# A decoder trunk on one core: modulation sums placed elsewhere

## The chip, the core and the metric

The kernel runs on one core of a Trainium2 chip. The metric is the device time of one execution in microseconds. Engines are named as in the profile: PE is TensorE, DVE is VectorE, ACT is ScalarE, POOL is GpSimd, SP is SyncE, which issues the DMAs here.

## The reference

Two layers on x of 256 rows by 1024. Each layer has a token mixer and a channel mixer, each of them with a modulation that is computed from one vector c:

```
mod = silu(c) @ w_ada[l] + b_ada[l]          # 1024 x 6144, split into sh1, sc1, g1, sh2, sc2, g2
h = x * (1 + sc1) + sh1
m = token_mixer(h)                           # h @ w_in (2816 columns: q k v hq hf hi hg pu), attention,
                                             # gated recurrence, causal pooling, then @ w_out
x = layer_norm(ALPHA * x + (1 + g1) * m) * ln1_g + ln1_b
h = x * (1 + sc2) + sh2
f = swiglu(h) (layer 0: FFN 2816)  or  moe(h) (layer 1: 8 experts of 3584, top 2)
x = layer_norm(ALPHA * x + (1 + g2) * f) * ln2_g + ln2_b
```

## The kernel before

The stages follow one another: mixer 1, dense SwiGLU, mixer 2, router, experts. The 256 rows are two blocks of 128 (NB = 2).

**Matmuls in fp32.** Each weight tile of 1 MB lands in a `raw` tile and is split by `split_half` into a high part `wh` (ScalarE, line 208) and a low part `wl` (line 209, on GpSimd or VectorE by the pattern LSUB). The input of a projection, `hT`, is split too (lines 313 and 314). Three matmuls make a product: high by high, high by low (lines 353 and 354 in the mixers, 924 and 925 in the dense stage) and low by high (356 and 927).

**The ring.** All weights come through `raw_tile`, a ring of RAW = 5 tiles (10 more where a mixer closes and during the experts), issued on SyncE's queue in program order (line 188). A tile is issued when its slot is free.

**Modulation pieces.** A piece is 512 columns of w_ada: two raw tiles (`ada_load`), eight matmuls on TensorE that sum them with the condition as stationary operand (line 270), a copy or an addition of the bias row on VectorE (lines 275 and 277), and then either four one-column matmuls that turn the sum into columns (`ada_cols`, line 283, with a small addition on VectorE, line 285), or one matmul that spreads it over the partitions and a ScalarE copy (`ada_gate_half`, lines 292 and 293). A sub-layer needs four shift and scale pieces (`queue_mod`) ahead of it and two gate pieces (`queue_gate`) behind it. The queue `bg` holds them, and `background(n)` takes n of them at that point of the program. In the mixers the points are given by BG (after the v, hv and u projections) and TURNS (turns of the loop over attention, projection and recurrence threads); in the dense stage FB = 2 are taken after each of the six chunks of the hidden width (256 and five of 512).

**First input.** `first_input(hf)` makes the input of mixer 1 for one half of the 1024 channels: two pieces, the affine coefficients, and `to_hT`, which transposes x (four 128x128 transposes per block, line 337), applies the affine step on ScalarE (line 342) and splits the result on VectorE. Two projections, f (columns from 1536) and q (from 0), take their steps between the halves; order on VectorE, ScalarE and TensorE is as written there (`manual_schedule`). Elsewhere a scheduler with its own costs sets each engine's order within the limits of the tiles and of `issue_after`, which puts an instruction behind another one of the same engine.

**Norms.** `resid_norm` adds the residual (lines 816 and 817), makes statistics, takes the reciprocal root on GpSimd (line 808) and normalises x in place on VectorE (line 822). Then the transposes of the next input follow. The norm's own scale and shift are folded into the affine coefficients for that input; for the residual path `new_x` applies them to x itself, two GpSimd rows per block (lines 855 and 856), behind the last reciprocal root.

## Time and profile before

| | |
|---|---|
| timed runs, median | 1532.04 us (1531.99, 1532.04, 1533.95) |
| profiled execution | 1529.82 us, span 1527.6 us |
| mean granted clock of TensorE | 0.944 |
| busy over the span | PE 91%, DVE 29%, ACT 21%, POOL 18% |
| mixer 1, with first input | 0 to 206.6 us |
| dense stage | 224.8 to 463.4 us |
| mixer 2 | 472.5 to 628.4 us |
| router, then experts | from 628.4 and 647.6 us |

A row of a timeline gives the start, the duration, the engine and line, what is written from what, and in brackets how long the engine idled before it and what released it. "wh", "wl" and "raw" are the weight tiles above, "acc" the sum of a piece, "rt" a half of `hT`, "bnrs" the reciprocal root. In tables by windows each engine's busy time is followed by its count of instructions; PE clock is the granted TensorE clock as a share of full speed (2.4 GHz; 0.5 is 1.2 GHz).

### The profile page before, as it was taken

How to read it: one execution, taken by the hardware profiler on the slowest of the kernel's cores; microseconds unless marked ns; L12 is line 12 of the kernel's file. 1: busy time of each engine (PE TensorE's matmuls, PEld its weight loads, DVE VectorE, ACT ScalarE, POOL GpSimd, SP SyncE). 2: the span in 40 equal slices, each digit the busy share in tenths (PEclk: the TensorE clock that was granted, in tenths of full speed). 3: DMA queues.
4: the chain of work that ended last, by engine and by line, in shares of the span. 5: the costliest groups of instructions: out<-in, count | busy, mean ns of one | idle time of the engine just before them, and what ended most of it. 6: DMA issues, size and time to landing. Idle time of an engine off the chain costs nothing.

```text
span 1527.6 us, 20906 instructions
## 1 busy us (share of the span) xinstructions
PE 1383.4 (91%) x8612; PEld 791.1 (52%) x8612; DVE 440.0 (29%) x748; ACT 320.2 (21%) x579; POOL 276.8 (18%) x154
## 2 busy tenths in 40 slices
PE   6889969999997988899978899899988999999994
PEld 3657758887875766743324344354434443435332
DVE  2555672322347656620000300002001200000303
ACT  2444434323324543211000100010000000001000
POOL 3443154544445532120000000000000000000001
PEclk7989989999998999899988799999999999999998
DMA  9756337766673532699999999999999999999994
GB/s 327 280 166 240 102 125 278 273 248 241 248 264 130 183 123 101 248 376 356 409 408 396 409 409 408 407 404 408 409 402 402 409 409 397 408 389 406 404 402 173
DMA packets 161094, 480.34 MB, mean 314 GB/s; under 512 B 9304, under 2 KB 14936, under 8 KB 160992
## 3 DMA queue, kind: packets, MB, share of 16 engines
q1 hardware_dynamic: 160992, 478.94, 82.2%
q8 instruction: 69, 1.13, 0.3%
q14 instruction: 33, 0.27, 0.0%
HBM read 477.86 MB, written 1.05 MB: 314 GB/s over the span
## 4 chain that ended last, share of the span: by engine, by line
issue 55%; PE 3%; POOL 1%; DMA 1%; DVE 0%; ACT 0%; POOLq 0%; DVEq 0%; ACTq 0%
PE psu L1206 1%; DMA raw<-in_ln_g_dram 1%; PE psx L1131 0%; PE pa L356 0%; PE pa L354 0%; PE pa L353 0%; POOL xa L1325 0%; PE pc L1034 0%; POOL xa L1323 0%; POOL rs L808 0%; ACT raw L1466 0%; DVE Sb L1122 0%; DVE off L1461 0%; ACT g L1041 0%; PE pb L1031 0%
## 5 line engine op out<-in xcount | busy, mean ns | idle before, releaser
L1206 PE MATMUL psu<-raw,xs 128*32 128x256 f32 (+4 forms) x3776 | 500.4, 432 | 21.0 <-DMA raw<-in_exp_w_dram 21.0
L1206 PEld LDWEIGHTS psu<-raw,xs 128*32 128x32 f32 (+2 forms) x3776 | 210.9, 127 | 298.5 <-issue 225.3
L209 POOL TENSOR_TENSOR wl<-raw,wh 128x1024 fp32r<-128x1024 f32 (+1 forms) x82 | 193.5, 2370 | 228.4 <-ACT wh L208 212.7
L1244 PE MATMUL psx<-raw,gT 128*32 128x512 f32 (+1 forms) x896 | 162.0, 636 | 15.0 <-DMA raw<-in_exp_w_dram 15.0
L208 ACT ACTIVATE wh<-raw 128x1024 fp32r<-128x1024 f32 (+1 forms) x130 | 131.2, 1033 | 192.6 <-DMA raw<-in_ffn_w_dram 78.8
L808 POOL TENSOR_TENSOR rs<-rs,mhalf 128x1 f32<-128x1 f32 x2 | 2.4, 1193 | 830.7 <-DVE rs L807 830.7
L353 PE MATMUL pa<-wh,rt 128*128 128x512 f32 (+1 forms) x296 | 119.2, 406 | 8.3 <-ACT wh L208 6.6
L354 PE MATMUL pa<-wh,rt 128*128 128x512 f32 (+1 forms) x296 | 116.6, 397 | 2.7 <-DVE rt L314 2.7
L209 DVE TENSOR_TENSOR wl<-raw,wh 128x1024 fp32r<-128x1024 f32 (+1 forms) x48 | 75.5, 1572 | 109.7 <-ACT wh L208 109.7
L1244 PE MATMUL psx<-raw,gTb 128*128 128x512 f32 x224 | 103.2, 612 | 1.1 <-DMA raw<-in_exp_w_dram 1.1
L356 PE MATMUL pa<-wl,rt 128*128 128x512 f32 (+1 forms) x296 | 100.2, 397 | 0.8 <-POOL wl L209 0.8
L1218 DVE TENSOR_TENSOR g<-g,psu 128x256 f32<-128x256 f32 (+2 forms) x32 | 15.2, 476 | 277.3 <-PE psu L1206 141.6
L1244 PEld LDWEIGHTS psx<-raw,gT 128*32 128x32 f32 (+1 forms) x896 | 37.8, 123 | 108.8 <-issue 87.3
L1214 ACT ACTIVATE g<-psu 128x256 f32<-128x256 f32 (+2 forms) x32 | 13.7, 427 | 302.8 <-PE psu L1206 302.8
L1244 PEld LDWEIGHTS psx<-raw,gTb 128*128 128x128 f32 x224 | 42.0, 194 | 60.1 <-issue 56.5
L353 PEld LDWEIGHTS pa<-wh,rt 128*128 128x128 f32 x296 | 58.7, 199 | 22.9 <-ACT wh L208 7.2
L1218 DVE TENSOR_TENSOR gb<-gb,psu 128x512 f32<-128x512 f32 x14 | 9.6, 688 | 211.5 <-PE psu L1206 211.5
L354 PEld LDWEIGHTS pa<-wh,rt 128*128 128x128 f32 x296 | 58.7, 198 | 14.1 <-DVE rt L314 3.9
L356 PEld LDWEIGHTS pa<-wl,rt 128*128 128x128 f32 x296 | 55.8, 197 | 14.0 <-POOL wl L209 2.3
L1229 ACT ACTIVATE gT<-psx 128x256 f32<-128x256 f32 (+2 forms) x32 | 13.6, 427 | 211.5 <-PE psx L1228 176.3
L924 PE MATMUL pb<-rt,wh 128*128 128x256 f32 x176 | 48.8, 298 | 9.3 <-DVE rt L313 6.8
L270 PE MATMUL pb<-raw,condw 128*32 128x512 f32 x384 | 49.0, 625 | 5.6 <-DMA raw<-in_w_ada_dram 5.6
(299 smaller groups left out, 1551.2 us busy)
## 6 DMA issues: line engine op xcount, KB each, us to landing
raw<-in_exp_w_dram SPq DMA_DIRECT2D x336, 1024.0 KB, 17.6
raw<-in_w_ada_dram SPq DMA_DIRECT2D x48, 1024.0 KB, 5.7
raw<-in_ffn_w_dram SPq DMA_DIRECT2D x31, 1024.0 KB, 6.9
raw<-in_w_in_dram SPq DMA_DIRECT2D x22, 1024.0 KB, 6.9
raw<-in_w_out_dram SPq DMA_DIRECT2D x8, 1024.0 KB, 5.0
raw<-in_ffn_w_dram SPq DMA_DIRECT2D x4, 512.0 KB, 4.8
t<-in_cst_dram SPq DMA_DIRECT2D x8, 192.0 KB, 2.5
x<-in_x_dram SPq DMA_DIRECT2D x2, 512.0 KB
```

The lines of the kernel that those rows point to most:

```text
L208: hl["act"] = act(h, ri, AF.Copy)
L209: hl["sub", eng] = (G if eng else V).tensor_tensor(l, ri, h.bitcast(F32), op=ALU.subtract)
L270: mm(ps[32 * j:32 * j + 32], condw[:, k, :], raws[k // 4][:, j, :], start=k < 4, stop=k >= 4)
L353: mm(ps, lH(a), rH(w), start=first and i == 0, stop=False)
L354: mm(ps, lL(a), rH(w), start=False, stop=False)
L356: mm(ps, lH(a), rL(w), start=False, stop=last and i == n - 1)
L924: mm(o_, wH[:, k, js], hT.H(4 * h + k0 + k, full), start=h + k0 + k == 0, stop=False)
L1206: mm(ps[self.rows(j)], self.of.xs[:, k0 + k, :], wv[:, k, o:o + w], start=k0 + k == 0, stop=k0 + k == KD - 1)
L1214: act(self.g[:, s_ * 512:s_ * 512 + min(512, self.F)], ps, AF.Silu)
L1218: V.tensor_mul(g, g, ps)
L1229: act(self.gT[:, b0:b0 + m, :], pt.rearrange("p (b s) -> p b s", b=m), AF.Copy)
L1244: mm(ps[self.rows(c)], self.gT[:, b, self.rows(j)], wv[:, i, hf * 512:hf * 512 + 512], start=seq == 0, stop=seq == n - 1)
```

## The change

There are three parts.

1. `first_input` is cut into four functions: load, sums, turn (transposes into the ps_c banks, which `to_hT` then reads) and apply. `mixer` calls them between single steps of the f and q projections; `proj(..., apart=True)` stops once after the load and split of its tiles.
2. `new_x` no longer issues its rows but puts the four of them into the queue `slow`; `aside()` takes one from it, on each odd turn of a mixer's loop and once before each of the 11 later column groups of the dense stage.
3. The dense stage takes one piece before its loop and one per chunk from the second on, between the w1 and the w3 matmuls, instead of two after each chunk. The pieces of gate 1 and of the second sub-layer of layer 1 are queued in mixer 2, which takes them by its BG and by five new TURNS; the last gate piece is left for the point after mixer 2.

```diff
--- before.py
+++ after.py
@@ -48,8 +48,7 @@
 
 
 BG = (0, 1, 0, 1)
-TURNS = ((10, 19, 20), ())
-FB = 2
+TURNS = ((10, 19, 20), (8, 12, 16, 19, 20))
 ORDER = "paprar"
 OUTORDER = ((0,), (1,), (3, 2))
 
@@ -329,12 +328,15 @@
         def L(self, k, s):
             return self.l[k // 4][:, k % 4, s]
 
-    def to_hT(src, AB_, dst, b, hf, after=None):
-
-        A, B = AB_
-        ps = ps_b()
+    def turned(src, hf, ps):
         for j in range(4):
             tr(ps[:, j * P:(j + 1) * P], src[:, (hf * 4 + j) * P:(hf * 4 + j + 1) * P], ident)
+        return ps
+
+    def to_hT(src, AB_, dst, b, hf, after=None, ps=None):
+
+        A, B = AB_
+        ps = ps or turned(src, hf, ps_b())
         bs = slice(b * P, (b + 1) * P)
         v = t2().rearrange("p (a t) -> p a t", a=4)
         for j in range(4):
@@ -417,7 +419,14 @@
         V.tensor_scalar(dst, ss, 1.0 / n, EPS, op0=ALU.mult, op1=ALU.add)
         G.tensor_tensor(dst, dst, mhalf[:, :dst.shape[1]], op=ALU.pow)
 
-    bg = []
+    bg, slow = [], []
+
+    def aside(n=1):
+
+        for _ in range(n):
+            if slow:
+                with tc.issue_after(hl["normed"].ins):
+                    slow.pop(0)()
 
     def background(n=1):
 
@@ -430,12 +439,16 @@
 
         W = w_in[l]
 
-        def proj(c0, n, ps):
+        def proj(c0, n, ps, apart=False):
+
 
             ps += [ps_a() for _ in range(NB)]
             pieces = [(0, lambda: piece(W, 0, D, c0, n))] if n == 256 else [(4 * h, lambda h=h: col_half(W, c0, n, h)) for h in range(2)]
             for h, load in pieces:
-                for k0, kk, wH, wL in load():
+                ws = load()
+                if apart:
+                    yield
+                for k0, kk, wH, wL in ws:
                     for b in range(NB):
                         part(ps[b], n, b, h + k0, kk, wH, wL)
                     yield
@@ -457,14 +470,26 @@
         psf, psq, psk, psv, psh, psu_ = [], [], [], [], [], []
         if inputs:
             with tc.manual_schedule(engines={E.DVE, E.Activation, E.PE}):
-                steps = [proj(1536, 512, psf), proj(0, 512, psq)]
-                for h in range(2):
-                    last = inputs(h)
-                    for g in steps:
-                        next(g)
-                        next(g)
-                for g in steps:
-                    run(g)
+                f_, q_ = proj(1536, 512, psf, True), proj(0, 512, psq, True)
+                load, sums, turn, apply_ = inputs
+                raws = load(0)
+                sums(0, 0, raws)
+                next(f_)
+                sums(0, 1, raws, turn)
+                apply_(0)
+                next(q_)
+                raws = load(1)
+                next(f_)
+                next(f_)
+                sums(1, 0, raws)
+                next(q_)
+                sums(1, 1, raws, turn)
+                next(q_)
+                apply_(1)
+                next(f_)
+                next(q_)
+                run(f_)
+                run(q_)
         else:
             psf += [ps_a() for _ in range(NB)]
             subs = [(4 * h + w[0],) + w[1:] for h in range(2) for w in col_half(W, 1536, 512, h)]
@@ -744,6 +769,8 @@
         while threads:
             for t_ in ORDER:
                 background(TURNS[l].count(turn))
+                if turn % 2:
+                    aside()
                 turn += 1
                 if t_ in threads and next(threads[t_], threads) is threads:
                     del threads[t_]
@@ -850,10 +877,9 @@
 
     def new_x(gb):
 
-        with tc.issue_after(row_stats.last.ins):
-            for b in range(NB):
-                G.tensor_tensor(x_t[b], x_t[b], gb[0], op=ALU.mult)
-                G.tensor_tensor(x_t[b], x_t[b], gb[1], op=ALU.add)
+        for b in range(NB):
+            for a, op in zip(gb, (ALU.mult, ALU.add)):
+                slow.append(lambda b=b, a=a, op=op: G.tensor_tensor(x_t[b], x_t[b], a, op=op))
 
     def queue_mod(l, sub, gk, bk):
         def go(which, hf):
@@ -878,18 +904,31 @@
 
     hT = Act()
 
-    def first_input(hf):
-        hT.new(hf)
-        for which in (1, 0):
-            ada_cols(0, which, hf, ada_acc(ada_load(0, which * D + hf * 512)))
+    def first_load(hf):
+        raws = [ada_load(0, which * D + hf * 512) for which in (1, 0)]
         if hf == 0:
             for b in range(NB):
                 nc.sync.dma_start(x_t[b], x[0, b * P:(b + 1) * P, :])
+        return raws
+
+    first_ps = []
+
+    def first_turn(hf):
+        hT.new(hf)
+        first_ps[:] = [turned(x_t[b], hf, ps_c()) for b in range(NB)]
+
+    def first_sums(hf, i, raws, between=None):
+        acc = ada_acc(raws[i])
+        if between:
+            between(hf)
+        ada_cols(0, 1 - i, hf, acc)
+
+    def first_apply(hf):
         affine_half(0, 0, None, None, hf)
         for b in range(NB):
-            last = to_hT(x_t[b], AB[0, 0], hT, b, hf)
-        return last
-
+            to_hT(None, AB[0, 0], hT, b, hf, ps=first_ps[b])
+
+    first_input = first_load, first_sums, first_turn, first_apply
     gate1 = queue_gate(0, 2)
     queue_mod(0, 1, LN["g1", 0], LN["b1", 0])
     acc = mixer(0, hT, first_input)
@@ -905,8 +944,7 @@
     hl["ph"] = 1
     gate2 = queue_gate(0, 5)
     queue_mod(1, 0, LN["g2", 0], LN["b2", 0])
-    gate1_ = queue_gate(1, 2)
-    queue_mod(1, 1, LN["g1", 1], LN["b1", 1])
+    background()
     yacc = [[ps_a() for _ in range(2)] for _ in range(NB)]
     full = slice(0, T)
     widths = [256] + [512] * (FFN // 512)
@@ -915,6 +953,10 @@
         nj = n // P
         pu = [(ps_b, ps_c)[j % 2]() for j in range(nj)]
         for wi, w in enumerate((ffn_w1, ffn_w3)):
+            if fc and wi:
+                background()
+            if fc + wi:
+                aside()
             for h in range(2):
                 for k0, kk, wH, wL in col_half(w[0], f0, n, h):
                     for j in range(nj):
@@ -952,7 +994,6 @@
         downs.append(down)
         if fc:
             downs.pop(0)()
-        background(FB)
         f0 += n
     downs.pop(0)()
     background(9)
@@ -964,6 +1005,8 @@
     new_x(gb)
 
     hl["ph"] = 2
+    gate1_ = queue_gate(1, 2)
+    queue_mod(1, 1, LN["g1", 1], LN["b1", 1])
     gate2 = queue_gate(1, 5)
     acc = mixer(1, hT)
     background(9)
```

In the rows below, taken from the order in which each engine's instructions stand, a line number of the changed kernel is that of the same code 1 lower in the pieces (269 for 270, 282 for 283) and 2 higher in the projections (355 for 353, 358 for 356).

The first place is TensorE in mixer 1, the end of the first projection steps, where the second half of the input is made. "raw,condw" is the sum of a piece, "quad,acc" its turn into columns, "cp,x" a transpose of x. Before:

```order
L356 MATMUL pa<-wl,rt 128x512 x2
L270 MATMUL pb<-raw,condw 32x512 x8
L283 MATMUL pb<-quad,acc 128x1 x4
L270 MATMUL pb<-raw,condw 32x512 x8
L283 MATMUL pb<-quad,acc 128x1 x4
L337 MATMUL pb<-cp,x_73 128x128 x4
L337 MATMUL pb<-cp,x_74 128x128 x4
L353 MATMUL pa<-wh,rt 128x512
L354 MATMUL pa<-wh,rt 128x512
L353 MATMUL pa<-wh,rt 128x512
L354 MATMUL pa<-wh,rt 128x512
```

After, from the fourth group of the first half:

```order
L358 MATMUL pa<-wl,rt 128x512 x2
L269 MATMUL pb<-raw,condw 32x512 x8
L282 MATMUL pb<-quad,acc 128x1 x4
L355 MATMUL pa<-wh,rt 128x512
L356 MATMUL pa<-wh,rt 128x512
```

and from the end of that step:

```order
L358 MATMUL pa<-wl,rt 128x512 x2
L269 MATMUL pb<-raw,condw 32x512 x8
L333 MATMUL pc<-cp,x_73 128x128 x4
L333 MATMUL pc<-cp,x_74 128x128 x4
L282 MATMUL pb<-quad,acc 128x1 x4
L355 MATMUL pa<-wh,rt 128x512
L356 MATMUL pa<-wh,rt 128x512
```

Before, the two sums, the two turns and the eight transposes stand together; after, four groups of projection matmuls (rows not shown between the two pieces) stand between the first sum and the second, and the transposes stand before the second turn, into the ps_c banks.

The second place is GpSimd from the dense stage to mixer 2. "bnrs" is a block's reciprocal root, x0 and x1 are the two blocks, t4 the rows of scale and shift, "wl" a low part of a weight tile. Before:

```order
L209 TENSOR_TENSOR wl_3631<-raw_3624,wh_3630 128x1024
L209 TENSOR_TENSOR wl_3773<-raw_3770,wh_3772 128x1024
L808 TENSOR_TENSOR bnrs_3699<-bnrs_3699,mhalf_87 128x1
L209 TENSOR_TENSOR wl_3783<-raw_3780,wh_3782 128x1024
L808 TENSOR_TENSOR bnrs_3736<-bnrs_3736,mhalf_87 128x1
L855 TENSOR_TENSOR x0_73<-x0_73,t4_3682 128x1024
L856 TENSOR_TENSOR x0_73<-x0_73,t4_3684 128x1024
L855 TENSOR_TENSOR x1_74<-x1_74,t4_3682 128x1024
L856 TENSOR_TENSOR x1_74<-x1_74,t4_3684 128x1024
L209 TENSOR_TENSOR wl_3843<-raw_3840,wh_3842 128x1024
```

After:

```order
L208 TENSOR_TENSOR wl_3502<-raw_3495,wh_3501 128x1024
L835 TENSOR_TENSOR bnrs_3570<-bnrs_3570,mhalf_87 128x1
L208 TENSOR_TENSOR wl_3640<-raw_3637,wh_3639 128x1024
L208 TENSOR_TENSOR wl_3650<-raw_3647,wh_3649 128x1024
L882 TENSOR_TENSOR x0_73<-x0_73,t4_3553 128x1024
L882 TENSOR_TENSOR x0_73<-x0_73,t4_3555 128x1024
L835 TENSOR_TENSOR bnrs_3607<-bnrs_3607,mhalf_87 128x1
L882 TENSOR_TENSOR x1_74<-x1_74,t4_3553 128x1024
L882 TENSOR_TENSOR x1_74<-x1_74,t4_3555 128x1024
L208 TENSOR_TENSOR wl_3710<-raw_3707,wh_3709 128x1024
```

Before, both roots stand ahead of all four x rows, and the first behind a weight's low part; after, the first root stands ahead of two weights' low parts, and the two rows of block 0 ahead of the second root. At the end of mixer 1 all four rows follow the second root in both, after with one low part of a weight behind the first row.

The third place is SyncE's issues in mixer 2, up to the constants of its pooling. Before:

```order
L188 DMA raw<-in_w_in_dram 128x4x512 x8
L188 DMA raw<-in_w_ada_dram 128x4x512 x2
L188 DMA raw<-in_w_in_dram 128x4x512 x2
L188 DMA raw<-in_w_in_dram 128x8x256
L188 DMA raw<-in_w_ada_dram 128x4x512 x2
L289 DMA brow<-in_b_ada_dram 1x512
L188 DMA raw<-in_w_out_dram 128x2x1024 x4
L188 DMA raw<-in_exp_w_dram 128x2x1024 x3
L761 DMA t_4726<-in_cst_dram 128x384
```

After, behind the same eight w_in tiles:

```order
L187 DMA raw<-in_w_ada_dram 128x4x512 x6
L288 DMA brow<-in_b_ada_dram 1x512
L187 DMA raw<-in_w_in_dram 128x4x512
L187 DMA raw<-in_w_ada_dram 128x4x512 x2
L187 DMA raw<-in_w_in_dram 128x4x512
L187 DMA raw<-in_w_ada_dram 128x4x512 x4
```

and from the w_out tiles on:

```order
L187 DMA raw<-in_w_out_dram 128x2x1024 x4
L288 DMA brow<-in_b_ada_dram 1x512
L187 DMA raw<-in_w_ada_dram 128x4x512 x2
L187 DMA raw<-in_exp_w_dram 128x2x1024
L788 DMA t_4707<-in_cst_dram 128x384
```

Before, two pairs of w_ada tiles stand between the w_in tiles and three expert tiles ahead of the constants; after there are seven pairs ahead of the w_out tiles (the seventh is not shown), three of them in a row ahead of one w_in tile, an eighth pair behind the w_out tiles, and one expert tile ahead of the constants.

## Rows read from the trace of the kernel before

**Rows 1.** Windows by stage: us, engines busy (count), PE clock, DMA share, GB/s.

```profile
66.20:206.60 140.40, 127.15 (x713) 98.44 (x711) 86.21 (x161) 61.04 (x123) 50.36 (x32) 0.94 0.48 161
...
224.80:463.40 238.60, 229.46 (x1584) 195.11 (x1584) 82.64 (x135) 80.21 (x96) 104.30 (x45) 0.97 0.71 256
...
472.50:628.40 155.90, 140.50 (x745) 111.48 (x746) 97.09 (x149) 71.48 (x141) 60.26 (x35) 0.98 0.38 127
...
647.60:700.00 52.40, 52.40 (x427) 21.16 (x428) 12.53 (x21) 10.63 (x21) 9.40 (x4) 1.00 0.89 338
...
700.00:1527.60 827.60, 765.86 (x4801) 316.25 (x4797) 104.41 (x174) 60.60 (x131) 5.81 (x6) 0.95 1.00 394
```

**Rows 2.** Windows of line 270 alone (sums of a piece), dense stage.

```profile
224.80:463.40 238.60, 23.08 (x192) 5.00 (x192) 0.97 0.71 256
```

**Rows 3.** Timeline of TensorE, single pieces: start, us, instruction, [idle before it].

```profile
274.47 1.92 PE L270 MATMUL pb<-raw,condw 128*32 128x512 f32 x16
...
277.39 0.95 PE L283 MATMUL pb<-quad,acc 128*128 128x1 f32 x8
...
536.23 1.10 PE L292 MATMUL pb<-acc,quad 128*128 128x512 f32 x2 [1.84 <-DVE acc L277]
```

**Rows 4.** Timeline of TensorE, first input of mixer 1, second half.

```profile
40.92 1.92 PE L270 MATMUL pb<-raw,condw 128*32 128x512 f32 x16
...
43.66 1.05 PE L283 MATMUL pb<-quad,acc 128*128 128x1 f32 x8 [0.81 <-DVE acc L275]
...
47.38 1.05 PE L283 MATMUL pb<-quad,acc 128*128 128x1 f32 x8 [0.81 <-DVE acc L275]
...
52.86 0.79 PE L353 MATMUL pa<-wh,rt 128*128 128x512 f32 x1 [3.50 <-ACT wh L208]
```

**Rows 5.** Timeline of TensorE, longest waits at and in the dense stage.

```profile
224.77 0.58 PE L924 MATMUL pb<-rt,wh 128*128 128x256 f32 x1 [6.75 <-DVE rt L313]
...
325.71 0.39 PE L924 MATMUL pb<-rt,wh 128*128 128x256 f32 x1 [2.50 <-DVE mod L285]
...
368.29 0.39 PE L924 MATMUL pc<-rt,wh 128*128 128x256 f32 x1 [2.19 <-ACT wh L208]
...
451.14 0.51 PE L353 MATMUL pa<-wh,X 128*128 128x512 f32 x1 [3.42 <-ACT wh L208]
```

**Rows 6.** Windows of 20 us in the dense stage.

```profile
320.00:340.00 20.00, 17.50 (x133) 17.30 (x133) 5.71 (x6) 7.30 (x7) 9.60 (x4) 0.91 0.95 361
...
440.00:460.00 20.00, 16.58 (x89) 10.95 (x88) 8.31 (x14) 3.19 (x4) 7.17 (x3) 0.91 0.71 260
```

**Rows 7.** Timeline of GpSimd and VectorE, mixer 1 to dense stage.

```profile
213.03 2.34 POOL L855 TENSOR_TENSOR x<-x,t 128x1024 f32<-128x1024 f32 x1
...
204.63 0.81 DVE L822 TENSOR_SCALAR x<-x,bnmv,bnrs 128x1024 f32<-128x1024 f32 x1 [0.66 <-POOL bnrs L808]
...
213.10 2.82 DVE L822 TENSOR_SCALAR x<-x,bnmv,bnrs 128x1024 f32<-128x1024 f32 x1 [0.67 <-POOL bnrs L808]
...
221.09 2.56 DVE L313 CAST rt<-t 128x512 fp32r<-128x512 f32 x1
...
224.29 0.42 DVE L313 CAST rt<-t 128x512 fp32r<-128x512 f32 x1
```

**Rows 8.** Timeline of GpSimd, VectorE and TensorE, dense stage to mixer 2.

```profile
464.79 1.54 POOL L808 TENSOR_TENSOR bnrs<-bnrs,mhalf 128x1 f32<-128x1 f32 x1
...
466.36 2.82 DVE L822 TENSOR_SCALAR x<-x,bnmv,bnrs 128x1024 f32<-128x1024 f32 x1 [0.44 <-POOL bnrs L808]
...
469.33 1.94 PE L337 MATMUL pb<-cp,x 128*128 128x128 f32 x8 [5.81 <-DVE x L822]
```

**Rows 9.** DMA issues on the page; columns: KB each, median us to landing.

```profile
raw<-in_w_ada_dram SPq DMA_DIRECT2D x48, 1024.0 KB, 5.7
```

**Rows 10.** Timeline of SyncE's issues, end of mixer 2 and start of experts.

```profile
571.24 7.02 SPq L188 DMA_DIRECT2D raw<-in_exp_w_dram  x3
...
614.50 45.12 SPq L188 DMA_DIRECT2D raw<-in_exp_w_dram  x16
```

## The prediction

> **What bounds the kernel now.** I read the windows by stage first. From 700 us on the DMA share is 1.00 and the expert weights stream at 394 GB/s to the end of the span [rows 1]: that stretch is a block of fixed length. Nothing in the change makes it shorter, so the time moves by as much as its start moves, which is the end of mixer 2 and of the router behind it. Ahead of it TensorE sets the pace: it is busy for 229.46 of 238.60 us in the dense stage, 140.50 of 155.90 in mixer 2 and 127.15 of 140.40 in mixer 1, with the DMA share at 0.71, 0.38 and 0.48 [rows 1]. So I count TensorE's work and its waits, stage by stage, and take the waits from its timeline. The profiled execution took 1529.82 us with a span of 1527.6; the median of the timed runs is 1532.04, and the sum of the differences is put on the median.
>
> **First input of mixer 1.** Before, the second half stands as a block on TensorE: two sums with their turns into columns, then eight transposes, and only then the next projection matmul. It lasts from 40.92 to 52.86, 11.94 us, of which 0.81, 0.81 and 3.50 are waits, 5.1 in all [rows 4]: for VectorE's copy twice, and once for the chain of ScalarE's affine step and its weights' high part. In the changed order each sum has four groups of six matmuls behind it, so the copies and the affine step run beside TensorE's work. No matmul is saved. The first matmul of the projections can't come much earlier, since it waits for the first w_in tile and the same chain as now. I take -4 of the 5.1, and leave 1 for a step of the new chain that is late (with transposes taken before the second turn, ScalarE may still hold a weight split). The ends are -1 (only one of the 0.81 goes) and -6 (all, and a clock that doesn't fall in the wait).
>
> **Mixer 1 to dense.** The four rows that scale and shift x now come from a queue, but at this place they still follow one another on GpSimd, with one weight split in between. Now the norm of block 1 takes 2.82 us beside such a row and 0.81 alone, a cast 2.56 beside and 0.42 alone [rows 7]. What makes the norm (its reciprocal root) and the first x row ready is not changed, so I take 0, with ends of -2 (the norm starts first) and +1.5.
>
> **Dense stage.** Line 270 stands there 192 times, 16 to a piece: 12 pieces [rows 2]; 6 are left. A piece costs TensorE 1.92 for its sum and 0.95 for its columns, or 1.10 for a gate's row [rows 3]; neighbours overlap a little, so 2.8: 6 x 2.8 = -16.8. The first of the remaining six now stands before the loop, and its 1.9 us fit into the 6.75 that TensorE waits at 224.77 [rows 5]: -1.9. Then the stalls: 2.50 for VectorE's mod behind the second piece of a pair, 2.19 and 3.42 for ScalarE's split of ffn_w tiles [rows 5] that stood behind four w_ada tiles in the one in-order ring. With one piece to a chunk the second of the pair is gone, and two tiles instead of four stand ahead of the weights: -8.1. In the two windows with such stalls the granted clock is 0.91 over 20 us [rows 6]; at 1.2 instead of 2.4 GHz that is 3.6 us, of which half is lost, so 1.8 a window: -3.6. Against that, a sum in the middle of the w3 block takes its PSUM bank from the same pool as the products, whose last reader is VectorE; the nearest row is the bare 0.81 wait for a copy [rows 4], and I take 0.5 in five chunks: +2.5, between 0 and 4. Together -27.9, ends -18 (most stalls stay) and -30.
>
> **Dense to mixer 2.** Now the reciprocal root of block 0 stands behind a weight split on GpSimd, starts at 464.79 and takes 1.54; the norm follows at 466.36, and TensorE waits 5.81 for it [rows 8]. The new order has it ahead of the splits: nearly 4 us of the 5.81 could go. But the two x rows of block 0 are moved ahead of block 1's root: that norm waits for them, and block 0's casts now run beside them at 2.56 instead of 0.42 [rows 7]. The casts feed the first projection, so about 2 of the 4 come back at once and another 1 with the second. I take -1, ends -5 and +2. The row has a cast at six times its time beside a GpSimd row [rows 7]. The Trainium skill (SBUF — State Buffer, section Who interferes with whom) says that such a pair isn't shared but locked, for the whole instruction, by the one that came first; this speaks against the new place of the rows here, and the trace agrees. By it block 1's norm, which no row overlaps any more, would be free and this term -3 instead of -1.
>
> **Mixer 2.** Five more pieces: 5 x 2.8 = +14.0. Of the two that are there now, one lets TensorE wait 1.84 for the sum [rows 3]. If every second new one does, that is 4.6; on the other hand mixer 1 has five pieces and idles 13.3 us, mixer 2 has two and idles 15.4 [rows 1], so pieces need add no wait. I take the middle, 2.3: +16.3. Ends: +6 (half of the 15.4 is filled by the new sums) and +23 (all five wait 1.84). On SyncE the six w_ada tiles now stand ahead of the w_in tile of the next group, and every queued weight waits for them.
>
> **The last piece.** The eighth follows the output projection, where nothing is left to hide it: 1.92 + 1.10, and 1 for VectorE's sum, which stands behind the row statistics of block 1: +4, ends +2.5 and +5.
>
> **Experts.** Before, three expert tiles are issued at 571.24, ahead of the constants, and 16 from 614.50 [rows 10]; after, one, since w_ada tiles take the slots. Two tiles at 394 GB/s are 5.3 us. But from 647.6 to 700 the DMA share is 0.89, which leaves 5.8 us idle while TensorE is busy throughout [rows 1]; the late tiles fit in there. I take 0, end +5.3.
>
> **Sum.** -4 + 0 - 27.9 - 1 + 16.3 + 4 + 0 = -12.6 against the profiled execution, and 1532.0 - 12.6 = 1519.4 us.
>
> **The rivals.**
> 1. The dense stalls stay. They may belong to the ring's five slots and not to the pairs: the DMA share there is 0.95 in one window and 0.71 in the other [rows 6], so the late tile isn't a matter of bandwidth. For it: a slot is free only when both splits have read it, and that isn't changed. Against it: two of three stalls come right behind the second piece of a pair. Without the -8.1 and -3.6 the sum is -0.9: 1531.1, no change.
> 2. The early expert loads are missed. For it: TensorE limits the start of the experts (busy 52.40 of 52.40) but may run dry later. Against: the idle DMA time of 5.8. The sum is then -7.3: 1524.7.
> 3. The x rows do come apart, so that norm and casts run free. At the first boundary this gives 2.0 + 2.1 + 2.1 and the low part of the split, alike 2.0: 8.3; at the second about 6 (norm, cast, low part): -14.3, a sum of -26.9 and 1505.1. Against it: the order on GpSimd, where all four still stand together; there the change doesn't do what it says.
> 4. Slower: in mixer 2 every piece waits for its own tiles. A w_ada tile takes 5.7 us from issue to landing [rows 9], and its slot is only released by TensorE's earlier sum, so with three pairs in a row the ring of five holds nothing but w_ada, and the sums stand in TensorE's in-order queue ahead of projection matmuls whose weights come later still. Price: 5 x 5.7 = 28.5 on top of 14.0, so 42.5 in place of 16.3; the sum is +13.6: 1545.6. It decides from a mixer 2 that is 28.9 us longer than now. For it: w_ada x6 in the new issue order. Against: a DMA share of 0.38 there, and mixer 1, where five pieces pass without such waits.
>
> **How the numbers follow.** The forecast has 0.45, its own range is 1511 to 1530 (the dense and mixer 2 terms at opposite ends); rival 1 has 0.17, rival 2 0.10, rival 3 0.08, rival 4 0.20. About 0.2% (3 us) is what a measurement can tell from no change. Faster by more than that: most of the forecast (0.42), rival 3, most of rival 2 (0.08) and a part of rival 1 (0.05): 0.63. Slower: rival 4 at full price and part-way, 0.18, and the upper ends of rival 1: 0.21. Within: 0.16. The range from 1506 to 1541 leaves out half of rivals 3 and 4.
>
> **What would show it.** In the changed profile: no wait over 1.5 us between the first projection matmuls; a dense stage of about 211 us with six pieces and no waits of 2 to 3 us; mixer 2 of about 172 us with no wait for a w_ada tile; four x rows together on GpSimd with a norm at 2.8 beside them at the first boundary; a full DMA from 700 us less the shift. I am wrong if mixer 2 gives back over 28.9 us, if waits for ScalarE's splits stay in the dense stage, or if the experts start earlier and the end doesn't move.

## The result and the profile after

The changed kernel took 1519.36 us in the median of six runs (1512.45 to 1524.68), against 1532.01 for the kernel before: a ratio of 0.9915 with an interval of 0.9886 to 0.9943. In a second series beside the experiments it took 1522.91 (1518.30 to 1523.76) against 1529.31, 0.9951 (0.9939 to 0.9963). So it is faster by less than 1%, clear of the noise: by 12.7 us in one series and 6.4 in the other. The changed kernel's own runs differ by 12.2 us in the first series, against 4.3 for the kernel before, and by 5.5 in the second, against 4.9. In the first series the granted clock of TensorE over the whole run mostly goes with the time: it is 0.959 in the fastest run and 0.951 in the slowest. The first profiled execution was the fastest of its series, with 1512.45 us and a span of 1510.7.

Windows by stage of that execution, columns as in [rows 1]:

```profile
65.50:203.90 138.40, 124.24 (x712) 96.43 (x711) 86.60 (x161) 60.34 (x121) 50.08 (x31) 0.98 0.50 171
...
222.50:430.00 207.50, 203.05 (x1420) 181.79 (x1421) 67.75 (x113) 78.47 (x91) 102.55 (x44) 0.99 0.66 228
...
470.50:607.00 136.50, 127.17 (x755) 95.47 (x753) 79.42 (x146) 56.01 (x115) 43.89 (x27) 1.00 0.58 199
...
628.60:700.00 71.40, 71.40 (x577) 26.87 (x576) 14.42 (x21) 11.54 (x22) 9.44 (x4) 1.00 0.96 371
...
700.00:1510.70 810.70, 746.08 (x4651) 308.50 (x4649) 104.16 (x173) 59.68 (x129) 5.81 (x6) 0.96 1.00 393
```

The dense stage was 238.6 us long with its clock at 0.97. From its first matmul at 222.46 to its last at 433.55 it is now 211.1 long, at 0.99; the second window leaves out its last 3.6 us. In mixer 2, counted from its k projection on, TensorE is busy 127.17 us of 136.50. From 628.6 to 700 the DMA share is 0.96, so the idle DMA time that [rows 1] showed at 0.89 is nearly used up, and from 700 on the expert weights stream as before at 393 GB/s.

The table puts the lengths of the stages beside one another. They are taken from the starts of the first and last projection matmuls of each stage, in the profiled executions; all but the first column are differences to the kernel before. "Again" is the same changed kernel, profiled once more in the second series; "pieces alone" and "mended" are experiments below.

| stretch, ends at | before | forecast | after | again | pieces alone | mended |
|---|---|---|---|---|---|---|
| first input, first matmul of the k projection | 66.21 | -4 | -0.8 | -0.4 | +0.5 | -2.2 |
| mixer 1, last matmul | 140.19 | 0 | -1.7 | -1.7 | -1.7 | -2.4 |
| first boundary, first dense matmul | 18.37 | 0 | +0.2 | +0.2 | +0.2 | -4.4 |
| dense stage, last matmul | 238.37 | -27.9 | -27.3 | -27.2 | -27.2 | -27.4 |
| second boundary, mixer 2's k projection | 40.63 | -1 | -3.7 | -1.1 | -3.1 | -9.4 |
| mixer 2, last matmul | 124.35 | +16.3 | +12.2 | +18.4 | +18.3 | +19.9 |
| last piece, router's transposes | 0.62 | +4 | +3.6 | +3.6 | +3.6 | 0.0 |
| router, first expert matmul | 18.90 | 0 | -1.5 | 0.0 | -1.5 | -0.1 |
| experts, end | 879.93 | 0 | +2.2 | +1.9 | +2.1 | +0.3 |
| sum | | -12.6 | -16.9 | -6.3 | -8.9 | -25.8 |

Two rows of the table also move where the change isn't. The first projection matmul starts anywhere between 24.7 and 27.6 us in kernels whose first input is untouched. From that matmul to the k projection it is 40.1 us before and 39.6 with the pieces alone, 39.1 and 39.4 in the two executions of the changed kernel, and 36.6 mended. Mixer 1 is 1.6 us shorter too in a kernel below that leaves it as it was (single pieces in the dense stage): from 66 to 204 us the clock is 0.98 there and in the changed kernel, and 0.94 before.

**First input.** The two 0.81 waits of [rows 4] are down to one and the 3.50 is down to 1.51, but new waits stand at the head. TensorE, ScalarE, GpSimd and VectorE in the changed kernel:

```profile
26.39 0.79 PE L355 MATMUL pa<-wh,rt 128*128 128x512 f32 x1 [4.75 <-DVE rt L312]
...
29.16 0.79 PE L356 MATMUL pa<-wh,rt 128*128 128x512 f32 x1 [1.97 <-DVE rt L313]
...
51.50 0.50 PE L355 MATMUL pa<-wh,rt 128*128 128x512 f32 x1 [1.51 <-ACT wh L207]
...
53.97 1.22 PE L358 MATMUL pa<-wl,rt 128*128 128x512 f32 x2 [1.28 <-POOL wl L208]
```

```profile
22.49 2.00 ACT L207 ACTIVATE wh<-raw 128x1024 fp32r<-128x1024 f32 x2 [18.71 <-DMA raw<-in_w_in_dram]
...
24.39 2.88 ACT L344 ACTIVATE t<-pc,B,A 128x128 f32<-128x128 f32 x8
```

```profile
23.62 4.93 POOL L208 TENSOR_TENSOR wl<-raw,wh 128x1024 fp32r<-128x1024 f32 x2 [18.46 <-ACT wh L207]
```

```profile
25.91 0.43 DVE L312 CAST rt<-t 128x512 fp32r<-128x512 f32 x1 [3.86 <-ACT t L344]
...
26.37 2.73 DVE L313 TENSOR_TENSOR rt<-t,rt 128x512 fp32r<-128x512 f32 x1
```

The first weights' high part now stands ahead of the affine step on ScalarE (22.49 and 24.39, where the step itself began at 22.27 before). So GpSimd already works on the low part while VectorE splits the input, and the low part of the input takes 2.73 us. TensorE waits 1.97 us for it before its second matmul, and at 51.50 and 53.97 another 1.51 and 1.28 for weights that ScalarE and GpSimd split too late.

**First boundary.** GpSimd, VectorE and TensorE, to be read against [rows 7] and the 6.75 of [rows 5]:

```profile
209.77 2.35 POOL L882 TENSOR_TENSOR x<-x,t 128x1024 f32<-128x1024 f32 x1 [1.19 <-PE pb L333]
```

```profile
208.87 0.80 DVE L849 TENSOR_SCALAR x<-x,bnmv,bnrs 128x1024 f32<-128x1024 f32 x1
...
214.11 2.73 DVE L313 TENSOR_TENSOR rt<-t,rt 128x512 fp32r<-128x512 f32 x1
...
216.76 2.57 DVE L312 CAST rt<-t 128x512 fp32r<-128x512 f32 x1
```

```profile
214.76 3.19 PE L269 MATMUL pb<-raw,condw 128*32 128x512 f32 x16 [0.28 <-ACT t L344]
...
222.46 0.58 PE L966 MATMUL pc<-rt,wh 128*128 128x256 f32 x1 [4.51 <-DVE rt L312]
```

The norm now takes 0.80 us, not 2.82: the first x row waited for the transposes, and the norm went ahead. The pieces alone do the same (0.81), and the rows alone keep 2.82, so it is the pieces' doing and not that of the new queue. But a cast still takes 2.57 beside such a row. Behind the sum of the first dense piece (214.76, 3.19 us, behind the transposes) 4.51 of the wait are left.

**Dense stage.** TensorE's waits between 224 and 428 as the view of waits groups them, by what it waited for; columns are total, times, longest:

```profile
PE pb L282 <- DVE acc L274: 2.8, 4, 0.7
...
PE pa L358 <- POOL wl L208: 0.8, 1, 0.8
...
PE pb L291 <- DVE acc L276: 0.7, 1, 0.7
```

None of the three long stalls of [rows 5] is left. There are five waits of 0.7 for the sums, nearer to the bare 0.81 of [rows 4] than to the 0.5 that I had taken.

**Second boundary.** GpSimd, VectorE and TensorE, to be read against [rows 8]:

```profile
431.15 0.55 POOL L835 TENSOR_TENSOR bnrs<-bnrs,mhalf 128x1 f32<-128x1 f32 x1 [6.01 <-DVE bnrs L834]
...
438.54 5.30 POOL L882 TENSOR_TENSOR x<-x,t 128x1024 f32<-128x1024 f32 x2
...
446.07 0.55 POOL L835 TENSOR_TENSOR bnrs<-bnrs,mhalf 128x1 f32<-128x1 f32 x1 [2.24 <-DVE bnrs L834]
```

```profile
431.74 0.81 DVE L849 TENSOR_SCALAR x<-x,bnmv,bnrs 128x1024 f32<-128x1024 f32 x1 [0.66 <-POOL bnrs L835]
...
441.53 2.58 DVE L312 CAST rt<-t 128x512 fp32r<-128x512 f32 x1
...
446.66 0.81 DVE L849 TENSOR_SCALAR x<-x,bnmv,bnrs 128x1024 f32<-128x1024 f32 x1 [0.66 <-POOL bnrs L835]
```

```profile
433.79 1.03 PE L333 MATMUL pb<-cp,x 128*128 128x128 f32 x8
...
438.91 0.54 PE L355 MATMUL pa<-wh,rt 128*128 128x512 f32 x1 [4.09 <-DVE rt L312]
...
441.67 0.80 PE L356 MATMUL pa<-wh,rt 128*128 128x512 f32 x1 [2.22 <-DVE rt L313]
```

Block 0's root runs as soon as it can, in 0.55 us, and the transposes start with no long wait ahead of them. Behind them the loss forecast is there: two x rows run from 438.54 to 443.84, VectorE's cast beside them takes 2.58, TensorE waits 4.09 and 2.22, and block 1's root comes at 446.07 after those rows.

**Last piece.** TensorE behind the output projection, and SyncE's issue of the only expert tile ahead of the pooling constants (three in [rows 10]):

```profile
607.30 1.92 PE L269 MATMUL pb<-raw,condw 128*32 128x512 f32 x16
...
610.22 1.12 PE L291 MATMUL pb<-acc,quad 128*128 128x512 f32 x2 [0.40 <-DVE acc L276]
```

```profile
560.79 0.37 SPq L187 DMA_DIRECT2D raw<-in_exp_w_dram  x1
```

### The profile page after: what moved, and what is told of

Read it like the earlier page. It is cut to its first block, busy times and chain, and to the rows that moved or that the text cites. A ratio compares the mean times of both kernels' runs of the same rounds, so it can differ in the third digit from the quotient of the medians.

```text
span 1510.7 us, 20910 instructions
## 1 busy us (share of the span) xinstructions
PE 1373.3 (91%) x8612; PEld 778.8 (52%) x8612; DVE 437.6 (29%) x748; ACT 321.2 (21%) x579; POOL 278.2 (18%) x154
## 4 chain that ended last, share of the span: by engine, by line
issue 55%; PE 3%; POOL 1%; DMA 1%; DVE 0%; ACT 0%; POOLq 0%
PE psu L1249 1%; DMA raw<-in_ln_g_dram 1%; PE psx L1174 0%; PE pa L356 0%; PE pa L358 0%; PE pa L355 0%; POOL xa L1368 0%; PE pc L1077 0%; POOL xa L1366 0%; POOL rs L835 0%; PE pb L1074 0%; ACT raw L1509 0%; PE pb L291 0%; DVE off L1504 0%; POOL raw L1510 0%
## 5 line engine op out<-in xcount | busy, mean ns | idle before, releaser
L355 PE MATMUL pa<-wh,rt 128*128 128x512 f32 (+1 forms) x296 | 116.7, 399 | 11.1 <-DVE rt L312 9.6
L356 PE MATMUL pa<-wh,rt 128*128 128x512 f32 (+1 forms) x296 | 115.2, 392 | 6.6 <-DVE rt L313 6.6
L208 DVE TENSOR_TENSOR wl<-raw,wh 128x1024 fp32r<-128x1024 f32 (+1 forms) x48 | 68.7, 1431 | 129.4 <-ACT wh L207 129.3
L355 PEld LDWEIGHTS pa<-wh,rt 128*128 128x128 f32 x296 | 57.1, 193 | 27.4 <-DVE rt L312 10.3
L966 PE MATMUL pc<-rt,wh 128*128 128x256 f32 x176 | 46.8, 287 | 4.5 <-DVE rt L312 4.5
```

The costliest lines, as they stand in the source:

```text
L208: hl["sub", eng] = (G if eng else V).tensor_tensor(l, ri, h.bitcast(F32), op=ALU.subtract)
L355: mm(ps, lH(a), rH(w), start=first and i == 0, stop=False)
L356: mm(ps, lL(a), rH(w), start=False, stop=False)
L966: mm(o_, wH[:, k, js], hT.H(4 * h + k0 + k, full), start=h + k0 + k == 0, stop=False)
```

## The experiments

Twelve kernels ran; all their ratios are against the kernel before on the same chip in the same series. The edits are shown in part, with `...` for what is left out.

**The whole change again.** 

> The changed kernel once more, beside the three parts alone. The first theory: the gain is the pieces taken out of the dense stage and the stalls that went with them, less what they cost in mixer 2, so the whole stays near 1519 us (1512 to 1525), and the parts alone add up to it within 4 us. Rival: the parts need each other (the new places of the sums only pay together with the new first input or the moved rows), so the whole is over 5 us better than the sum of its parts. Its profile should also show where runs of this kernel differ by up to 12 us: if in the stretch before the experts, the start of the expert matmuls moves from 628.6; if in the experts, only the time from there to the end (882.1 us in the first profile) changes.

1522.91 us, 0.9951 (0.9939 to 0.9963). Up to the end of the dense stage the two executions agree within 0.5 us. They part in three places: 2.6 us at the second boundary, 6.3 in mixer 2 and 1.6 in the router. The experts differ by 0.3. Most of this is TensorE's clock. Windows of the second boundary, first in the execution of 1512.45 us and then in the one of 1523.16, and of mixer 2 in the latter (columns as in [rows 1]; mixer 2 of the first is the third row of the windows above):

```profile
433.60:470.70 37.10, 27.35 (x115) 21.36 (x114) 29.73 (x27) 20.12 (x36) 23.79 (x10) 0.91 0.36 114
...
434.10:473.50 39.40, 29.69 (x114) 23.09 (x113) 28.45 (x27) 20.59 (x37) 23.29 (x11) 0.83 0.33 107
...
473.50:616.30 142.80, 131.38 (x755) 96.98 (x753) 81.90 (x145) 55.24 (x114) 42.16 (x27) 0.96 0.56 190
```

At the boundary TensorE idles for 9.7 us in both, and only its clock differs, 0.91 and 0.83. In mixer 2 the same 755 matmuls keep it busy for 127.17 us at 1.00 and for 131.38 at 0.96: 4.2 of the 6.3. In the router the idle time is 5.2 in both, and the clock 0.70 and 0.64. The faster execution has no stretch at 1.2 GHz from 447 to 616 us. The slower one has one from 453.4, one from 511.4, right behind the wait of 4.08 below, and one from 559.2. Up to the first of them TensorE's rows are the same in both, so why the clock falls there isn't shown.

The other 2.2 us of mixer 2 are one wait, around its second sum. GpSimd, VectorE and TensorE, first in the execution of 1512.45 us:

```profile
504.82 2.47 POOL L208 TENSOR_TENSOR wl<-raw,wh 128x1024 fp32r<-128x1024 f32 x1 [0.36 <-ACT wh L207]
```

```profile
503.30 1.78 DVE L686 TENSOR_TENSOR X<-E,kqz 128x256 f32<-128x256 f32 x3 [2.88 <-ACT E L678]
...
505.01 0.68 DVE L276 TENSOR_TENSOR acc<-pb,brow 128x512 f32<-128x512 f32 x1
...
505.83 1.10 PE L291 MATMUL pb<-acc,quad 128*128 128x512 f32 x2 [1.92 <-ACT wh L207]
```

and in the one of 1523.16 us:

```profile
507.44 2.53 POOL L208 TENSOR_TENSOR wl<-raw,wh 128x1024 fp32r<-128x1024 f32 x1
```

```profile
506.31 3.94 DVE L686 TENSOR_TENSOR X<-E,kqz 128x256 f32<-128x256 f32 x3 [2.88 <-ACT E L678]
...
510.17 0.68 DVE L276 TENSOR_TENSOR acc<-pb,brow 128x512 f32<-128x512 f32 x1
...
511.00 1.62 PE L291 MATMUL pb<-acc,quad 128*128 128x512 f32 x2 [4.08 <-DVE acc L276]
```

Ahead of the bias sum of a gate piece VectorE has three products of the recurrence. They take 1.78 us in one execution and 3.94 in the other, and TensorE waits 1.92 or 4.08 for the sum. The instructions and their order are the same, but not the start of GpSimd's next weight split: in the first it waits 0.36 us for ScalarE's high part and starts when the products are nearly done, in the other the high part is ready and the split runs beside the products. The other profiles with this order agree: 1.79 where GpSimd waits for the high part (rows held back), 3.93 or 3.94 where it doesn't (pieces alone, eighth piece, mended). Of the 12 us between runs, this pair of profiles places about 10, of which some 8 are clock and 2 this wait; what the other runs did is not shown.

**The three parts alone.** The first input:

```diff
-                steps = [proj(1536, 512, psf), proj(0, 512, psq)]
-                for h in range(2):
-                    last = inputs(h)
...
+                f_, q_ = proj(1536, 512, psf, True), proj(0, 512, psq, True)
+                load, sums, turn, apply_ = inputs
```

> Only the first input is changed; rows of scale and shift and all pieces stand as before. The prediction had -4 us for it; the first profile of the whole change shows -0.8 at the first matmul of the k projection (65.45 instead of 66.21), because the low parts of the first weights on GpSimd now run beside VectorE's splits of the input (2.73 us for one instead of 0.69). By that theory this kernel gains 0 to 2.5 us (1529.5 to 1532) and its k projection starts 0 to 1.5 us earlier. By the prediction's own step it gains 4 (1528) and k starts at about 62.

1529.91 us, 0.9999 (0.9990 to 1.0008): nothing. k starts 0.95 earlier, mixer 1 ends 1.49 earlier, and the dense stage is 1.8 longer. The rows through the queue:

```diff
-        with tc.issue_after(row_stats.last.ins):
-            for b in range(NB):
-                G.tensor_tensor(x_t[b], x_t[b], gb[0], op=ALU.mult)
...
+            for a, op in zip(gb, (ALU.mult, ALU.add)):
+                slow.append(lambda b=b, a=a, op=op: G.tensor_tensor(x_t[b], x_t[b], a, op=op))
```

> Only the rows of scale and shift go through the new queue. Theory: they still stand together on GpSimd, the norm at the first boundary keeps its 2.8 us, and the only shift is block 1's reciprocal root behind block 0's rows at the second boundary, which costs 0 to 2.5 us: 1532 to 1534.5, no change. Rival: the queue does spread them and norms and casts run free: 8 to 14 us faster (1518 to 1524), and the gain of the whole change is mostly this.

1531.57 us, 1.0014 (1.0000 to 1.0027): no change, at most 0.3% slower, with runs that spread over 11.5 us. Its first boundary is as long as before to 0.01 us. At the second one block 0's rows stand ahead of block 1's root, as in the whole change. TensorE idles 12.6 us there and not 11.1, which the length doesn't show (0.5 shorter), since TensorE's own work took 2.1 less. The places of the pieces:

```diff
-TURNS = ((10, 19, 20), ())
-FB = 2
+TURNS = ((10, 19, 20), (8, 12, 16, 19, 20))
...
+            if fc and wi:
+                background()
```

> Only the places of the modulation pieces are changed (6 instead of 12 in the dense stage, 8 instead of 2 around mixer 2). Theory: dense stage with its boundary about 30 us shorter, mixer 2 and the last piece about 16 longer, so 1518 to 1523 us, all or nearly all of the gain of the whole change. Rival (the stalls of the dense stage belong to the ring and not to the pairs): the dense stage only loses the work of six pieces, 15 to 17 us, mixer 2 gives it back, and the time is 1530 to 1533.

1518.04 us, 0.9926 (0.9914 to 0.9939). All of the gain is here; the whole change is 4.9 us behind it in the same series (0.9951 against 0.9926; the intervals meet at 0.9939). Its second boundary is 2.0 shorter than that of the whole change profiled beside it, and TensorE idles 8.3 us there and not 9.7. In its order block 1's root still stands ahead of the x rows. So block 0's rows ahead of that root cost 1.4 us of waits there, and 1.5 in the kernel with the rows alone. The other 3 us between the medians were not placed. That the root of block 0 comes ahead of the weights' low parts is also owed to the pieces: it is so in the order of this kernel and not in that of the rows alone.

**Twelve pieces in the dense stage, but not in pairs.**

```diff
-FB = 2
+FB = 1
...
+            if wi:
+                background()
```

> The kernel before, with all twelve pieces still in the dense stage, but one between each chunk's w1 and w3 matmuls and one after the chunk, instead of two after it. Theory (the stalls of 2.50, 2.19 and 3.42 us belong to the pair: the second sum right behind the first, and four w_ada tiles in a row in the ring): they go and the clock stays up, the stage from its first matmul to the transposes of the next input falls from 244.6 to 231 to 237 us, and the time by 8 to 12 us (1518 to 1522). Rival (they belong to the number of w_ada tiles that pass through five slots in that stage): the stage stays within 3 us of 244.6 and the time within 3 us of the kernel before.

1521.93 us, 0.9949 (0.9936 to 0.9962), inside what the first theory gave, at its upper edge. The stretch named in the expectation is 233.6 and not 244.6, inside the range too. But 5.0 of these 11.0 are the dense stage, and 6.0 are the wait ahead of the transposes, of which all but 2.2 come back by mixer 2's k projection. TensorE's waits there, in the same view:

```profile
PE pb L292 <- DVE acc L277: 2.6, 2, 1.9
...
PE pb L283 <- DVE acc L275: 2.1, 3, 0.7
```

The waits for weight splits (3.42, 2.19) and for the mod addition (2.50) are gone, with the same number of w_ada tiles through the same five slots. So the stalls belong to the pair. What single pieces keep are 4.7 us of waits for the sums, the longest 1.9.

**The affine step first.**

```diff
-                next(f_)
                 sums(0, 1, raws, turn)
                 apply_(0)
+                next(f_)
                 next(q_)
```

> The new first input alone, with the affine step of the first half put ahead of the split of the first projection weights on ScalarE. Theory: the affine step starts at about 22.0 us instead of 24.4, GpSimd has no weight to split yet while VectorE splits the input, so the second of these splits takes 0.69 instead of 2.73 us, TensorE's wait of 1.97 us before its second matmul goes, and the k projection starts 2 to 3 us earlier than in the new first input as it stands (65.3 in that kernel): 62.5 to 63.5. Rival: the chain of the first weight tile decides, and the k projection starts at 65 again or later. The time itself is expected at 1527 to 1530 by both, since the part as it stands lost its 1.5 us again by the end of the dense stage.

1528.68 us, 0.9995 (0.9986 to 1.0004). k starts at 63.02, 3.2 earlier than before and 2.2 earlier than with the part as it stands. From the first projection matmul to k it is 37.0 us here, 40.0 with the part as it stands and 40.1 before. VectorE and TensorE:

```profile
24.09 0.69 DVE L314 TENSOR_TENSOR rt<-t,rt 128x512 fp32r<-128x512 f32 x1
...
25.99 0.79 PE L356 MATMUL pa<-wh,rt 128*128 128x512 f32 x1 [4.40 <-ACT wh L208]
...
26.58 0.63 PE L357 MATMUL pa<-wh,rt 128*128 128x512 f32 x1
```

The low part of the input takes 0.69 us again, and no wait stands ahead of the second matmul. That shows where most of the forecast's -4 went. The time is the same as before, as both theories said: in this kernel 0.9 goes at the first boundary and 1.7 in the dense stage.

**The rows held back.** With the pieces moved, the first input as before, and the rows put behind the latest weight split on GpSimd, from the second chunk on (the edit is shown against the changed kernel):

```diff
-                with tc.issue_after(hl["normed"].ins):
+                with tc.issue_after(hl["sub", True].ins):
                     slow.pop(0)()
...
-            if fc + wi:
+            if fc:
                 aside()
```

> The new places of the pieces, and the rows of scale and shift held back on GpSimd behind weight splits of the second chunk of the dense stage, and of the first projection threads of mixer 2; the first input as before. Theory (rival 3 of the prediction, now made to happen): norm, casts and low parts at the two boundaries run free of these rows, 8 us and up to 6 us: 1504 to 1510, against about 1518 with the pieces alone. Rival: VectorE waits for ScalarE's affine steps instead (2.9 us for eight), so only 3 to 6 us of it reach TensorE: 1512 to 1515.

1515.50 us, 0.9918 (0.9903 to 0.9934): just above the rival's range. It is 2.5 below the pieces alone, which were timed in the series before; the two intervals overlap. The theory had 8 and up to 6 us at the two boundaries; in the profiles they are 4.5 and 6.5 shorter than with the pieces alone. VectorE at the first one:

```profile
211.09 0.80 DVE L830 TENSOR_SCALAR x<-x,bnmv,bnrs 128x1024 f32<-128x1024 f32 x1
...
213.85 0.43 DVE L312 CAST rt<-t 128x512 fp32r<-128x512 f32 x1 [1.22 <-ACT t L341]
```

But the dense stage was 4.3 us longer. VectorE and TensorE, 20 us into it:

```profile
239.46 5.10 DVE L313 TENSOR_TENSOR rt<-t,rt 128x256 fp32r<-128x256 f32 x2
...
244.48 2.35 DVE L208 TENSOR_TENSOR wl<-raw,wh 128x1024 fp32r<-128x1024 f32 x2
...
245.75 0.50 PE L937 MATMUL pb<-rt,wl 128*128 128x256 f32 x2 [3.63 <-DVE wl L208]
```

Two low parts of products took 5.10 us here, where they take 0.75 with the pieces alone. GpSimd had one of the held rows at 236.92 and two weight splits behind it, from 239.35 to 244.3, beside these low parts; with the pieces alone it was idle then. So the split of the next weights on VectorE came late: a wait of 3.63.

**The eighth piece inside mixer 2.**

```diff
-TURNS = ((10, 19, 20), (8, 12, 16, 19, 20))
+TURNS = ((10, 19, 20), (8, 12, 16, 19, 20, 26))
```

> The new places of the pieces, and the eighth piece taken at a turn inside mixer 2 instead of after its output projection. Theory: the 3.6 us that it costs there become 2.8 us of work beside the recurrence or less, and the expert tiles no longer queue behind its two w_ada tiles: 1 to 4 us faster than with the pieces alone (about 1514 to 1517). Rival: TensorE waits in mixer 2 for one more sum or its tiles, 4 us and more: 1518 or above.

1516.05 us, 0.9911 (0.9896 to 0.9925), 2 us below the pieces alone, which were timed in the series before (the intervals overlap). Mixer 2 is not longer (+18.4 against +18.3): TensorE idles 0.7 us less in it, and its clock is 0.98 and not 0.96, which hides the work of one piece more. The 3.6 behind it are gone, and the experts take 879.7 instead of 882.1. SyncE issues three expert tiles ahead of the constants again, so the late expert loads look like these 2 us. That isn't quite shown: with the rows held back SyncE issues one such tile, as with the pieces alone, and the experts take 880.4.

**Other turns in mixer 2.** On top of the late rows (the edit is shown against that kernel):

```diff
-(8, 12, 16, 19, 20))
+(2, 5, 17, 20, 23, 26))
```

> The pieces in mixer 2 at other turns (2, 5, 17, 20, 23, 26: all eight inside the mixer), on top of the late rows. Theory: TensorE's wait for the second gate piece's sum in mixer 2 (1.9 us in one execution, 4.1 in others) comes from VectorE, where that sum stands behind three products of the recurrence that take 1.8 or 3.9 us together, as GpSimd works beside them or not; here both gate sums stand ahead of these products, so mixer 2 from its k projection to its last matmul is 3 to 6 us shorter than with late rows alone (139.2 us there in its profiled execution) and the runs spread by less than 8 us: 1508 to 1513. Rival: the sums only move the wait to the next piece (the third now stands behind the same products), no shorter mixer 2 and a time of 1514 to 1518.

1514.16 us, 0.9887 (0.9869 to 0.9904). Its time lies where the rival put it, just above the theory's range, and mixer 2 was 147.0 us, 7.7 longer than with the late rows alone. All of the 7.7 is TensorE's busy time, by one piece more and a clock of 0.97 and not 1.00; it idles 11.6 us in both. The wait moved; VectorE and TensorE:

```profile
484.03 0.42 DVE L531 TENSOR_TENSOR t<-pa,rotMH 128x256 f32<-128x256 f32 x1 [7.11 <-POOL t L533]
...
486.66 2.04 PE L291 MATMUL pb<-acc,quad 128*128 128x512 f32 x2 [4.39 <-DVE acc L276]
```

VectorE sat idle for 7.11 us, waiting for GpSimd in the rotation, and the gate's sum stood behind that. So my theory of the place was too narrow: it isn't these three products, but whatever stands ahead of the sum in VectorE's order.

**Twelve single pieces with late rows,** without and with the mended first input. The dense loop is that of the single pieces, and in the second kernel the first piece stands ahead of the loop:

```diff
+            if wi:
+                background()
+            if fc:
+                aside()
...
+    background()
     yacc = [[ps_a() for _ in range(2)] for _ in range(NB)]
```

> All twelve pieces stay in the dense stage, one at a time; the rows of scale and shift are held back as in the late-rows kernel; the first input as before. Theory (count in mixer 2 costs as much as in the dense stage, plus waits there; the stalls went with the pairs and the slow norms with the rows): pairs apart alone is at 1522; the late rows take another 4.5 us at the first boundary and 6 at the second: 1510 to 1514, with a mixer 2 of about 125 us from its k projection. Rival: the place in mixer 2 is what pays, so this stays 3 us or more behind the late rows with eight pieces in mixer 2 (1515.5): 1518 to 1521.

1513.95 us, 0.9885 (0.9866 to 0.9903). As good as the moved pieces with other turns in the same series (1514.16): the place in mixer 2 isn't what pays. Mixer 2 was 130.9 us and not 125: against the single pieces without late rows TensorE idles 2.3 us more in it and has a clock of 0.96, not 0.99. The late rows now fall into it, but that they are the cause isn't shown. The first boundary is 7.5 us shorter than before, where moved pieces and late rows gave 4.4.

> As the kernel with twelve single pieces and late rows, with the first input's new order and its affine step ahead of the weight split, and the first of the twelve ahead of the dense loop, in the wait at the first boundary. Theory: 3 us from the first input and about 2 from the piece hidden at the boundary, all of it ahead of a dense stage that is bound by TensorE: 1505 to 1509. Rival: as with the new first input alone, the dense stage ends no earlier, since its last weights come when the ring lets them: within 2 us of the kernel without it (1510 to 1514).

1512.46 us, 0.9873 (0.9853 to 0.9894): the rival's number. Of 5 us expected from the first input and the hidden piece, 1.5 arrived. The first boundary is 3.0 longer than without a piece in it (13.8 and 10.9): with the rows held back there is no wait left that would hide the piece.

**The whole change, mended.** The affine step first, the eighth piece at turn 26, and the rows held back, one to a chunk:

```diff
-            if fc + wi:
+            if fc and wi:
                 aside()
```

> The whole change with three places mended: the affine step of the first input ahead of the first weights' split, the rows of scale and shift held back behind weight splits (one to a chunk in the dense stage), the eighth piece at a turn inside mixer 2. Theory (the parts add up, since TensorE's waits set the time up to the experts): from the pieces alone (1518) it loses 2 for the eighth piece, 3 for the rows and 1 to 2 for the first input: 1509 to 1513, with k at 63 us, a first boundary of about 14 us and the experts' stretch back at 880. Rival: what is gained ahead of the dense stage runs into weights that the ring brings no earlier, as where the dense stage of the late-rows kernel was 4.4 us longer than with the pieces alone: 1514 to 1517.

1506.68 us (1502.57 to 1507.21), 0.9828 (0.9812 to 0.9843): faster than both kernels, and below the theory's range. Here the first boundary is 4.4 and the second 9.4 us shorter and the dense stage keeps its -27.4: what the rows gave at the boundaries isn't taken back, as it was in the first kernel with late rows. The slow low parts are here too (5.15 us for two), but the wait for the split behind them is 2.3 and not 3.6, and the clock of the stage is 1.00 and not 0.98. Two things differ there, one row to a chunk instead of two and the earlier end of the first input; which of them did it is open.

## Why the prediction was right

The direction and the size were right, 1519.4 forecast and 1519.36 measured in the first series; the second series gave 1522.9, still inside the likeliest case's own range. Such a close hit is more than the steps earned: some of their errors cancel, and part of the spread between executions is the clock. The own range of 1511 to 1530 is also narrower than the terms that it names: -30 with +6 gives 1507, and -18 with +23 gives 1536. Two of the signs named did not come: waits over 1.5 us stayed between the first projection matmuls (1.97 and 1.51), and no norm of 2.8 stood at the first boundary.

1. **First input, -4: measured -0.8 and -0.4.** This term failed in size. The mechanism was there and was paid back at the same place: between the first projection matmul and k TensorE idles 5.75 us, where it idled 5.94. I had named the risk (ScalarE may still hold a weight split) and put 1 us on it. It cost 2.2 by the start of k, and 3.0 counted from the first projection matmul, shown by the kernel with the affine step first. The cost came not on ScalarE but one step on: the earlier split woke GpSimd while VectorE worked on the input.
2. **First boundary, 0: measured +0.2.** Right, though not by what I had written: the norm did go free (0.80), and the casts that follow kept their 2.6. With the rows held back the stretch is 4.4 shorter where the first dense piece stands in it, and 7.5 shorter where no piece does (twelve single pieces with late rows). So rival 3's price of 8.3 there was nearly right for the kernel before, and the first piece is hidden only as long as the rows slow the casts.
3. **Dense stage, -27.9: measured -27.3 twice.** The six pieces, the hidden first one, the stalls of the pairs and their clock are all where they were put: TensorE's busy time falls by 22.6 us (forecast 22.3, for the work and the clock) and its idle time by 4.7 (forecast 5.6, stalls less new waits). The kernel with single pieces separates work from stalls: with twelve pieces the stage falls by 5.0. The forecast's stalls and clock, -11.7, with the 4.7 of short waits that are left there, would make -7.0.
4. **Second boundary, -1: measured -3.7 and -1.1.** The gain by the earlier root and the loss by the x rows are both in the rows: TensorE's idle time falls from 11.1 to 9.7 us in both executions. The 2.6 between them are its clock, 0.91 and 0.83, and 0.83 is that of the kernel before. At 446.66 block 1's norm takes 0.81 us, free of any row. By the rule of the lock in the Trainium skill (SBUF — State Buffer, section Who interferes with whom), which I had weighed there at -3, it would be; the trace agrees. The -3 itself did not come: at the clock of before the term is -1.1.
5. **Mixer 2, +16.3: measured +12.2 and +18.4.** Work was right: at a clock of 1.00 TensorE is busy for 127.2 us, 14.1 more than before. The waits were not. I had put 2.3 on new ones; one sum alone has 1.92 or 4.08, but other waits are shorter, and the idle time, 11.3 before, is 9.3 in one execution and 11.4 in the other. The second execution's +18.4 is then 14.1 of work and 4.2 of a lower clock, which I had put at nothing here. That the term lies between the two is luck.
6. **Last piece, +4: measured +3.6.**
7. **Experts, 0: measured +2.** I said that two late tiles fit into 5.8 us of idle DMA time. With one early tile the experts take 881.9 to 882.1 us in three profiles and 880.4 in a fourth, with three tiles 879.7 to 880.8 in all; so rival 2 was right in kind and worth 2 us at most instead of 5.3, and what makes the fourth differ is open.

Rival 4 didn't come: no wait of TensorE in mixer 2 was for a w_ada tile. Rival 1 fell with the single pieces. Rival 3 was right as a price list and wrong as to what the change does.

## What to carry to other kernels

Work that is taken out of a saturated stage gives back its own time and the stalls that it caused there. Here the stage gave back 5.0 us when its pieces were taken one at a time, with all of them still in it, and 27.3 when six were moved out as well. Such a kernel should separate the two before anything is moved to another stage. Before a difference between two executions is put down to an order, compare TensorE's busy time, idle time and granted clock over the stretch: of the 10 us between two executions here, some 8 were clock. An instruction that only fills in is worth as much as the in-order queue in front of it allows: look at what stands ahead of its successor on VectorE, and not at the gap on TensorE. A queue that is meant to delay work must be tied to something later on the same engine; with a limit that names an instruction of VectorE these GpSimd rows stayed where they were at the first boundary, and two of them went ahead of a root at the second.

## What the runs showed of the hardware

Three products of 128x256 on VectorE take 1.78 us in one execution and 3.94 in the next, with the same program: 3.94 where GpSimd's weight split runs beside them. A cast of 128x512 takes 0.43 us alone and 2.6 beside a GpSimd row, and a 128x1024 norm 0.81 and 2.82. I hadn't expected that moving a split on ScalarE by 2 us could slow VectorE fourfold (0.69 to 2.73) by way of GpSimd. With the same matmuls and the same idle time, TensorE's stretch at the second boundary takes 37.1 us at a granted clock of 0.91 and 39.4 at 0.83. The runs of one program spread over 4 us for the kernel before and over 12 for the change in the first series. Why isn't shown: the pieces alone spread over 4.0, and the rows alone, with no piece moved, over 11.5.
